# Mixture-of-experts stage of a hybrid encoder block: one result row per token, summed by the second expert's fetch

## The chip, the cores and the metric

The kernel runs on one core of one Trainium2 chip. The metric is the device time of one execution in microseconds. Three runs of the kernel before took 2249.4, 2248.95 and 2247.48 us, median 2248.95.

The engines are called by their usual short names: PE is TensorE, DVE is VectorE, ACT is ScalarE, POOL is GpSimd, SP is SyncE. A name such as L1415 is a line of the kernel.

## The reference

One layer over 2048 tokens of 1024 float32 values, `h`:

- `proj = h @ w_in`, 2048 columns: q, k, v of 8 heads and the input u of a bidirectional state-space model (S5).
- Neighbourhood attention over a 32 x 64 grid of tokens, S5 with GELU and GLU, both concatenated and multiplied by `w_out`; then `h = LayerNorm(alpha * h + mix)`.
- A hierarchical mixture of experts: each token chooses one of 8 groups, and in that group the two best of 8 experts. With gates g1 and g2:

```
hid_e = silu(x @ w_gate[e]) * (x @ w_up[e])      # 1024 -> 512
y     = g1 * (hid_e1 @ w_down[e1]) + g2 * (hid_e2 @ w_down[e2])
out   = LayerNorm(alpha * h + y)
```

Every token thus has two experts, both of the same group, and `alpha * h` has to be added once.

## The kernel before, in words

Work goes through five stages.

1. **Projection.** `w_in` comes in 16 chunks of 128 columns, in the hand-written `order`. SP loads a chunk (`load_w1`, L468) into a ring `rawp` of two raw buffers; ACT makes the high part (L445) and DVE the low part (L447) of the split that the three matmuls of `mm3` (L106 to L108) use. For each chunk four blocks `nb` of 512 tokens are computed, 24 matmuls each, into four PSUM tiles (`psA`). `evac` copies a block out, one block later: for the first four chunks (12 to 15, the u columns) ACT copies it (L489) into a staging tile of a pool with two buffers, and SP stores that to `ud` (L490). Chunk `n + 2` is loaded while chunk `n` is multiplied. At `n == 2` DVE fills one raw buffer with an out-of-range number (`sent`), and POOL's DMA queue copies it over the whole table `tab` (L755). The setup of S5 runs beside all this on DVE.
2. **Attention and S5**, then 3. **GLU, `w_out`, LayerNorm and router**, 128 tokens at a time. The normalized rows go to `hd` in device memory. `router_a` (L1149) finds the two experts `ef`, their gates and an entry `ent` of four words per choice: token row, output row, gate, factor of the residual. `router_b` (L1222) counts ranks within each expert and scatters the entries into `tab`, 96 slots (`SL`) for each expert; slots that stay unused keep the out-of-range number. For the last tile the index of the first expert's rows is taken from a matmul (`idx0`, L1244), so that the first gather (L1212) need not wait for `tab`.
4. **Experts.** Iteration `e` of the loop runs on POOL the gather of 96 rows of `hd` for expert e + 3 (L1212, six buffers `hg`), on PE gate and up of expert e, the transposes of expert e + 1 and down of expert e - 1; on ACT the residual scaling of expert e - 1 (L1400), on DVE the multiplication by the gate and the addition to the scaled rows (L1413); POOL scatters the rows to `yd` (L1415). `yd` has two rows per token: the first choice writes `alpha * h + g1 * y1`, the second `g2 * y2` (factor 0 for the residual). Weights come through a ring of 1 MB halves loaded by SP (L1106) in the order `seq_`; ACT (L1311) and DVE (L1317) split them for `mm3`. In iterations e = 6 to 26 POOL scatters one more small list (L1530), for a loop over experts with more than 96 tokens (L1535), which makes no turn with these inputs.
5. **Final stage.** SP loads both rows of 128 tokens (L1582, 1 MB a tile, 16 tiles, all issued at once), DVE adds them (L1593), ACT forms mean and variance (L1595, L1596) and the root (L1597), DVE scales (L1601 to L1603), two tiles later in program order, and POOL's queue stores (L1604).

The order of instructions on each engine is the order of the program; a DMA waits in its issuing engine's queue until its semaphores are there.

Of the kernel before, what the change touches and what calls it, by code (L numbers as in the profile page):

```python
# [12 lines left out]
F32 = mybir.dt.float32  # L13
F32R = mybir.dt.float32r
BF16 = mybir.dt.bfloat16
I32 = mybir.dt.int32
# [10 lines left out]
NE, DE = 64, 512  # L27
# [6 lines left out]
SPL = 1  # L34
NOT0 = 1 << 12
SL = 96
NBX = -(-SEQ // SL) - 1
NROW = SL * (NBX + 1)

# [33 lines left out]
def encoder_block(ctx: ExitStack, tc: tile.TileContext, A, out, dbg=None):  # L73
# [20 lines left out]
    md = dram.tile([G, C, 8, 128], F32, name="md")  # L94
    tbd = dram.tile([128, 2, G, 256], F32, name="tbd")
    hd = dram.tile([SEQ, DM], F32, name="hd")
    yd = dram.tile([2 * SEQ, DM], F32, name="yd")
    tab = dram.tile([NROW * NE, 4], I32, name="tab")
    lst = dram.tile([64, 4], I32, name="lst")

# [11 lines left out]
    GP.iota(io8, pattern=[[1, 8]], base=0, channel_multiplier=0, allow_small_or_imprecise_dtypes=True)  # L112
    io64 = const.tile([128, 64], F32, name="io64")
    GP.iota(io64, pattern=[[1, 64]], base=0, channel_multiplier=0, allow_small_or_imprecise_dtypes=True)
    tokf = const.tile([128, 16, 2, 2], I32, name="tokf")
    GP.iota(tokf, pattern=[[128, 16], [0, 2], [0, 2]], base=0, channel_multiplier=1)
    GP.iota(tokf[:, :, 1, 1:2], pattern=[[128, 16], [0, 1]], base=SEQ, channel_multiplier=1)
    alf = const.tile([128, 2], F32, name="alf")
    V.memset(alf[:, 0:1], ALPHA)
    V.memset(alf[:, 1:2], 0.0)  # L120
# [627 lines left out]
    for n, ch in enumerate(order):  # L748
        if n < 2:
            continue  # L750
        if n == 2:
            nfill = NROW * NE * 4 // 2048
            sent = rawp.tile([128, nfill], I32, name="sent", tag="raw")
            V.memset(sent, OOB)
            GP.dma_start(tab.rearrange("(p a b) w -> p a (b w)", p=128, a=16), sent[:, None, :].to_broadcast([128, 16, nfill]))  # L755
        hl = nxt
        for nb in range(4):
            ps = psA.tile([128, 512], F32, name="pp")
            for k in range(8):
                mm3(ps, (hl[:, 0, k, :], hl[:, 1, k, :]), (xs[nb][0][:, k, :], xs[nb][1][:, k, :]), k == 0, k == 7)  # L760
            if nb == SPL and n + 1 < len(order):
                nxt = split_chunk(order[n + 1])
            if nb == (max(2, SPL) if n == 2 else 0) and n + 2 < len(order):
                load_w1(order[n + 2])
            if n == 15:

                if nb == 0:
                    KT = [buf16([128, 2, ROWS, GW], F32R)]
                    QT = buf16([128, 2, SEQ], F32R)
                    load_k(0, 0)  # L770
                    load_k(0, 1)
                    load_q(0, 0)
                if nb == 1:
                    bts = buf16([128, 4, 2, 512])
                    KT.append(buf16([128, 2, ROWS, GW], F32R))
                    load_b()
                if nb == 2:
                    mixT = [buf16([128, 8, 512])]
                    for u in range(3):
# [304 lines left out]
        return A["w_" + nm][e].rearrange("(p j) f -> p j f", j=4 if nm == "down" else 8)  # L1084

    seq_ += [("gate", 0), ("up", 0)]
    for e in range(1, NE):
        seq_ += [("gate", e), ("up", e), ("down", e - 1)]
    seq_.append(("down", NE - 1))
    loaded, nsplit = [], [0]  # L1090
    ring, free, held = [], [], None

# [56 lines left out]
    def router_a(n, pr, res):  # L1149
# [48 lines left out]
        TS(dn, e2, 1.0, gs, ALU.add, ALU.mult)  # L1198
        ent = cw.tile([128, 2, 4], I32, name="ent", bufs=4)
        gt = ent.bitcast(F32)  # L1200
        V.tensor_copy(ent[:, :, 0:2], tokf[:, n])
        V.tensor_copy(gt[:, :, 3], alf)
        yield
        V.reciprocal(gt[:, 0, 2:3], dn)
        yield
# [5 lines left out]
    def gather(tb, hgt):  # L1211
        GP.indirect_dma_start(out=hgt[:SL], out_offset=None, in_=hd[:],  # L1212
                              in_offset=bass.IndirectOffsetOnAxis(ap=tb[:SL, 0:1], axis=0),
                              bounds_check=SEQ - 1, oob_is_err=False)

    def rank_m(oo):
        pr2 = psR.tile([128, 2, 64], F32, name="pr2")
# [4 lines left out]
    def router_b(pr2, ef, o2, oo, ent, val, n):  # L1222
# [16 lines left out]
            yield  # L1239
        row = cw.tile([128, 2], I32, name="row", bufs=4)  # L1240
        STT(row, rks, 64.0, ef, ALU.mult, ALU.add)
        yield
        if n == 15:
            TS(idx0[:SL], p0[:SL, 0:1], float(NOT0), None, ALU.add)  # L1244
# [167 lines left out]
    def down_out(tb, hgt, py, no_dep=True):  # L1412
        STT(hgt[:SL], py[:SL], tb[:SL, 2:3].bitcast(F32), hgt[:SL], ALU.mult, ALU.add)  # L1413
        GP.memset(spacer, 0.0)
        d = GP.indirect_dma_start(out=yd[:], out_offset=bass.IndirectOffsetOnAxis(ap=tb[:SL, 1:2], axis=0),  # L1415
                                  in_=hgt[:SL], in_offset=None, bounds_check=2 * SEQ - 1, oob_is_err=False)
        if no_dep:
            for o in ybufs:
                tc.declare_no_dep(d.ins, o.ins, reason="different rows")
            ybufs.append(d)  # L1420

    def down(hhl, get, tb, hgt, no_dep=True):
# [5 lines left out]
    def piece(nm, e, extra):  # L1428


        i = 4 * seq_.index((nm, e))
# [48 lines left out]
    for t_ in hg[1:]:  # L1480
        V.memset(t_, 0.0)
    for k in (1, 2):
        gather(tabs[:, k], hg[k])
    hid = None
    gb = None
    last = None
    for e in range(NE + 1):
# [4 lines left out]
            SY.dma_start(lng, A["ln2_g"].to_broadcast([128, DM]))  # L1492
            SY.dma_start(lnb, A["ln2_b"].to_broadcast([128, DM]))
        if e + 3 < NE:
            gather(tabs[:, e + 3], hg[(e + 3) % NHG])
        out_ = (tabs[:, e - 1], hg[(e - 1) % NHG]) if e else None
        if e < NE:
            get, after = piece("gate", e, {})
            pgt = up_mm(xhl, get, "g", after)
# [35 lines left out]
    with tc.For_i(0, nv, 1) as it:  # L1535
# [5 lines left out]
        SY.dma_start(tb[:SL], tab[bass.ds(rb_, SL, 64), :])  # L1541
        gather(tb, hg[0])
        xhl = trans_x(hg[0])

        nld = [0]

# [28 lines left out]
    fw = pf.enter_context(tc.tile_pool(name="fw", bufs=4))  # L1575
    ys = {}

    fy = [buf16([128, 2, 2, DM]) for _ in range(8)]

    def load_y(n):  # L1580
        ys[n] = fy[n // 2][:, n % 2]
        SY.dma_start(ys[n], yd.rearrange("(k t) d -> t k d", k=2)[128 * n:128 * n + 128])  # L1582

    eps = fp.tile([128, 1], F32, name="eps")
    V.memset(eps, EPS)
    for n in range(16):
        load_y(n)
    fin = {}
    for n in range(19):
        if n < 16:  # L1590
            y = ys.pop(n)
            h, junk = y[:, 0], y[:, 1]
            TT(h, h, junk, ALU.add)  # L1593
            mu, va = (fw.tile([128, 1], F32, name=f"m{c}") for c in "uv")
            S.activation(junk, h, AF.Copy, scale=-1.0 / DM, accum_out=mu)  # L1595
            S.activation(junk, h, AF.Square, bias=mu, accum_out=va)  # L1596
            S.activation(va, va, AF.Sqrt, bias=eps, scale=1.0 / DM)  # L1597
            fin[n] = h, mu, va
        if 2 <= n < 18:
            h, mu, va = fin.pop(n - 2)  # L1600
            V.reciprocal(va, va)  # L1601
            STT(h, h, mu, lng, ALU.add, ALU.mult)
            STT(h, h, va, lnb, ALU.mult, ALU.add)  # L1603
            GP.dma_start(out[128 * (n - 2):128 * (n - 2) + 128, :], h)  # L1604
    pf.close()
    if dbg:
        loc = dict(qd=qd, kd=kd, ud=ud, zd=zd, hd=hd, yd=yd, tab=tab)
# [66 lines left out]
```

## Time and profile before

| | before |
|---|---|
| median of three runs | 2248.95 us |
| the profiled execution's own time | 2250.54 us |
| its span in the trace | 2248.8 us |
| mean granted clock of TensorE, of full speed | 0.965 |
| PE busy | 2086.3 us (93%) |
| DVE busy | 1954.8 us (87%) |
| ACT busy | 1385.7 us (62%) |
| POOL busy | 524.8 us (23%) |
| DMA moved | 634.04 MB, mean 282 GB/s |

Busy times are from the profile's first section and overlap one another. A high share says only that an engine is full somewhere; which engine sets the pace in a stage has to be read from that stage. "DMA share" in a stretch is the mean busy share of the core's 16 DMA engines. In a row of a timeline the bracket at the end is the engine's idle time before the instruction and what ended it. "To landing" is the time from the issue of a DMA to its completion.

### The profile page before, as it was taken

How to read it: one execution, taken by the hardware profiler on the slowest of the kernel's cores; microseconds unless marked ns; L12 is line 12 of the kernel's file. 1: busy time of each engine (PE TensorE's matmuls, PEld its weight loads, DVE VectorE, ACT ScalarE, POOL GpSimd, SP SyncE). 2: the span in 40 equal slices, each digit the busy share in tenths (PEclk: the TensorE clock that was granted, in tenths of full speed). 3: DMA queues.
4: the chain of work that ended last, by engine and by line, in shares of the span. 5: the costliest groups of instructions: out<-in, count | busy, mean ns of one | idle time of the engine just before them, and what ended most of it. 6: DMA issues, size and time to landing. Idle time of an engine off the chain costs nothing. (4 is left out here: it accounts for less than half of the span.)

```text
span 2248.8 us, 31008 instructions
## 1 busy us (share of the span) xinstructions
PE 2086.3 (93%) x10653; PEld 1578.4 (70%) x10653; DVE 1954.8 (87%) x3573; ACT 1385.7 (62%) x1950; POOL 524.8 (23%) x408
## 2 busy tenths in 40 slices
PE   8999899999999999969999999999999999999940
PEld 6887677866666788856777777777777777777730
DVE  6976668999996778878999999999999999999967
ACT  4232221147778321127888888888888888888855
POOL 0001110010000011232244444443333333333211
PEclk9999899999999999979999999999999999999975
DMA  7435566599865433369999999999999999999647
GB/s 223 125 125 172 207 239 213 184 302 289 245 177 157 154 113 117 121 249 323 369 381 381 385 387 387 379 378 378 378 379 378 374 377 377 380 381 379 250 168 296
DMA packets 219887, 634.04 MB, mean 282 GB/s; under 512 B 39280, under 2 KB 119120, under 8 KB 170576
## 3 DMA queue, kind: packets, MB, share of 16 engines
q1 hardware_dynamic: 187424, 550.07, 68.3%
q0 software_dynamic: 32016, 81.40, 10.9%
q8 instruction: 85, 1.39, 0.3%
q10 hardware_dynamic: 288, 0.57, 0.1%
q14 instruction: 74, 0.61, 0.1%
HBM read 557.93 MB, written 100.26 MB: 293 GB/s over the span
## 5 line engine op out<-in xcount | busy, mean ns | idle before, releaser
L1317 DVE TENSOR_TENSOR b<-b,b 128x1024 fp32r<-128x1024 f32 x544 | 640.8, 1216 | 47.5 <-ACT b L1311 38.3
L1311 ACT ACTIVATE b<-b 128x1024 fp32r<-128x1024 f32 x544 | 576.0, 1059 | 144.1 <-PE pg L108 55.6
L1415 POOL DMA_INDIRECT yd<-hg,tabs x64 | 306.3, 4786 | 718.2 <-DVE hg L1413 689.1
L106 PE MATMUL pp<-b,whl 128*128 128x512 f32 (+1 forms) x520 | 210.0, 404 | 9.1 <-DVE b L447 8.3
L106 PE MATMUL pu<-b,xhl 128*96 128x512 f32 x512 | 206.0, 402 | 0.0
L108 PE MATMUL pg<-b,xhl 128*96 128x512 f32 x512 | 204.2, 399 | 1.7 <-DVE xhl L447 1.7
L106 PE MATMUL pg<-b,xhl 128*96 128x512 f32 x512 | 203.0, 396 | 2.6 <-ACT xhl L445 2.6
L107 PE MATMUL pp<-b,whl 128*128 128x512 f32 (+1 forms) x520 | 203.3, 391 | 1.2 <-DVE b L447 1.2
L108 PE MATMUL pp<-b,whl 128*128 128x512 f32 (+1 forms) x520 | 203.4, 391 | 0.5 <-DVE whl L447 0.5
L107 PE MATMUL pg<-b,xhl 128*96 128x512 f32 x512 | 202.6, 396 | 0.0
L106 PE MATMUL py<-b,hhl 128*96 128x512 f32 x504 | 202.1, 401 | 0.0
L108 PE MATMUL pu<-b,xhl 128*96 128x512 f32 x512 | 201.4, 393 | 0.0
L107 PE MATMUL pu<-b,xhl 128*96 128x512 f32 x512 | 200.9, 392 | 0.0
L108 PE MATMUL py<-b,hhl 128*96 128x512 f32 x504 | 198.0, 393 | 0.0
L107 PE MATMUL py<-b,hhl 128*96 128x512 f32 x504 | 197.5, 392 | 0.0
L1317 DVE TENSOR_TENSOR b<-half,b 128x1024 fp32r<-128x1024 f32 x132 | 157.1, 1216 | 11.3 <-ACT b L1311 8.9
L1311 ACT ACTIVATE b<-half 128x1024 fp32r<-128x1024 f32 x132 | 139.8, 1059 | 32.6 <-PE pg L108 11.5
L106 PEld LDWEIGHTS pp<-b,whl 128*128 128x128 f32 x520 | 99.7, 192 | 28.8 <-ACT b L445 8.3
L1317 DVE TENSOR_TENSOR b<-slot,b 128x1024 fp32r<-128x1024 f32 x92 | 109.0, 1216 | 7.8 <-ACT b L1311 6.1
L108 PEld LDWEIGHTS pp<-b,whl 128*128 128x128 f32 x520 | 99.5, 191 | 21.9 <-DVE whl L447 1.0
L107 PEld LDWEIGHTS pp<-b,whl 128*128 128x128 f32 x520 | 99.6, 192 | 21.3 <-DVE b L447 1.9
L108 PEld LDWEIGHTS pg<-b,xhl 128*96 128x96 f32 x512 | 83.3, 163 | 38.7 <-DVE xhl L447 2.8
(385 smaller groups left out, 4324.8 us busy)
## 6 DMA issues: line engine op xcount, KB each, us to landing
b<-in_w_up_dram SPq DMA_DIRECT2D x93, 1024.0 KB, 10.5
b<-in_w_gate_dram SPq DMA_DIRECT2D x90, 1024.0 KB, 8.6
b<-in_w_down_dram SPq DMA_DIRECT2D x88, 1024.0 KB, 9.1
half<-in_w_down_dram SPq DMA_DIRECT2D x23, 1024.0 KB, 8.8
half<-in_w_gate_dram SPq DMA_DIRECT2D x21, 1024.0 KB, 8.6
half<-in_w_up_dram SPq DMA_DIRECT2D x21, 1024.0 KB, 10.6
slot<-in_w_gate_dram SPq DMA_DIRECT2D x16, 1024.0 KB, 8.6
slot<-in_w_down_dram SPq DMA_DIRECT2D x16, 1024.0 KB, 9.2
```

Of the source, the lines that this page charges most:

```text
L106: T.matmul(o, l[0], r[0], start=start, stop=False)
L107: T.matmul(o, l[0], r[1], start=False, stop=False)
L108: T.matmul(o, l[1], r[0], start=False, stop=stop)
L1311: S.activation(wh[k % len(wh)][:, 0], src, AF.Copy, scale=1.0)
L1317: TT(hl[:, 1], src, hl[:, 0].bitcast(F32), ALU.subtract)
L1415: d = GP.indirect_dma_start(out=yd[:], out_offset=bass.IndirectOffsetOnAxis(ap=tb[:SL, 1:2], axis=0), in_=hgt[:SL], in_offset=None, bounds ...
```

## The change

- The experts are visited in the order `EO`: the first expert of each of the 8 groups, then the second of each, and so on. A token's two experts are then at least eight positions apart.
- `yd` has one row per token. It is filled once, at `n == 2` of the projection, with the bit pattern of the out-of-range number, which as float32 is a denormal next to zero; the transfer is issued by ACT, and `sent` grows from 264 to 1024 columns.
- `router_b` finds out which of the two choices comes second in the new order (`sec`; an overflowing slot counts as later). Its residual factor is 1 instead of alpha, and its entry's second word is the token's row; the first choice has a row out of range there.
- From e = 8 on, after the gather, `gather_sum` fetches rows of `yd` into `hg` for those slots that are a second choice, so that the residual scaled by 1 is the sum of the first expert. The scatter goes to the token's row for both choices.
- The final stage loads one row per token, 0.5 MB a tile, has no addition on DVE, and runs the scaling one tile after the statistics, not two.

The core of the diff:

```diff
+EO = [8 * (s % 8) + s // 8 for s in range(NE)]
...
-    yd = dram.tile([2 * SEQ, DM], F32, name="yd")
+    yd = dram.tile([SEQ, DM], F32, name="yd")
...
-            sent = rawp.tile([128, nfill], I32, name="sent", tag="raw")
+            sent = rawp.tile([128, DM], I32, name="sent", tag="raw")
             V.memset(sent, OOB)
...
+            S.dma_start(yd.rearrange("(p a) d -> p a d", p=128), sent.bitcast(F32)[:, None, :].to_broadcast([128, 16, DM]))
...
-    for e in range(1, NE):
-        seq_ += [("gate", e), ("up", e), ("down", e - 1)]
+    for s_ in range(1, NE):
+        seq_ += [("gate", EO[s_]), ("up", EO[s_]), ("down", EO[s_ - 1])]
...
-        V.tensor_copy(ent[:, :, 0:2], tokf[:, n])
-        V.tensor_copy(gt[:, :, 3], alf)
+        V.tensor_copy(ent[:, :, 0], tokf[:, n])
...
+    def gather_sum(tb, hgt):
+
+        return GP.indirect_dma_start(out=hgt[:SL], out_offset=None, in_=yd[:],
+                                     in_offset=bass.IndirectOffsetOnAxis(ap=tb[:SL, 1:2], axis=0),
+                                     bounds_check=SEQ - 1, oob_is_err=False)
...
+        sec = cw.tile([128, 2], F32, name="sec")
+        TS(sec, rks, SL - 0.5, 64.0, ALU.is_gt, ALU.mult)
+        yield
+        TT(ef, sec, ef, ALU.add)
+        yield
+        TT(sec, ef, ef[:, ::-1], ALU.is_gt)
+        yield
+        TS(ent.bitcast(F32)[:, :, 3], sec, 1.0 - ALPHA, ALPHA, ALU.mult, ALU.add)
+        STT(ent[:, :, 1], sec, -float(OOB), toko[:, n], ALU.mult, ALU.add)
...
-        d = GP.indirect_dma_start(out=yd[:], out_offset=bass.IndirectOffsetOnAxis(ap=tb[:SL, 1:2], axis=0),
-                                  in_=hgt[:SL], in_offset=None, bounds_check=2 * SEQ - 1, oob_is_err=False)
+        d = GP.indirect_dma_start(out=yd[:], out_offset=bass.IndirectOffsetOnAxis(ap=tb[:SL, 0:1], axis=0),
+                                  in_=hgt[:SL], in_offset=None, bounds_check=SEQ - 1, oob_is_err=False)
...
-            gather(tabs[:, e + 3], hg[(e + 3) % NHG])
+            gather(tabs[:, EO[e + 3]], hg[(e + 3) % NHG])
+        if 8 <= e < NE:
+            d = gather_sum(tabs[:, EO[e]], hg[e % NHG])
+            for o in ybufs[-6:]:
+                tc.declare_no_dep(d.ins, o.ins, reason="rows of other groups")
+            sums.append(d)
...
-        SY.dma_start(ys[n], yd.rearrange("(k t) d -> t k d", k=2)[128 * n:128 * n + 128])
+        SY.dma_start(ys[n], yd[128 * n:128 * n + 128, :])
...
-    for n in range(19):
+    for n in range(18):
         if n < 16:
-            y = ys.pop(n)
-            h, junk = y[:, 0], y[:, 1]
-            TT(h, h, junk, ALU.add)
+            h = ys.pop(n)
+            junk = fw.tile([128, DM], F32, name="junk", bufs=1)
...
-        if 2 <= n < 18:
-            h, mu, va = fin.pop(n - 2)
+        if 1 <= n < 17:
+            h, mu, va = fin.pop(n - 1)
```

What it moves shows in the instruction streams at three places. ACT in the projection, around the place where `sent` is set; `us` is the staging tile, `pp` a PSUM tile, `whl` the split chunk. Before:

```order
L445 ACTIVATE whl<-raw 128x1024 [waits DMAHW7_49,DVE_49,PE_49]
L489 COPY us<-pp 128x64x8 [waits DMAHW0_49,Activation_49]
L489 COPY us<-pp 128x64x8 [waits DMAHW1_49,Activation_49]
L489 COPY us<-pp 128x64x8 [waits DMAHW3_49,PE_49,Activation_49]
L445 ACTIVATE whl<-raw 128x1024 [waits DMAHW2_49,DVE_49]
L489 COPY us<-pp 128x64x8 [waits DMAHW4_49,PE_49,Activation_49]
```

and now:

```order
L445 ACTIVATE whl<-raw 128x1024 [waits DMAHW7_49,DVE_49,PE_49]
L489 COPY us<-pp 128x64x8 [waits DMAHW0_49,Activation_49]
L489 COPY us<-pp 128x64x8 [waits DMAHW1_49,Activation_49]
L757 DMA yd<-sent 2048x1x1024 [waits DVE_49]
L489 COPY us<-pp 128x64x8 [waits DMAHW3_49,PE_49,Activation_49]
L445 ACTIVATE whl<-raw 128x1024 [waits DMAHW2_49]
L489 COPY us<-pp 128x64x8 [waits DMAHW4_49,PE_49,Activation_49]
```

The fill stands between two copies out of PSUM and waits for DVE (the memset of `sent`).

SP's queue at the same place; `raw` is a buffer of the chunk ring, DMASW0 belongs to the table's fill on POOL's queue and, in the second piece, DMAHW5 to the fill of `yd`. Before:

```order
L490 DMA ud<-us 1024x1x64 [waits Activation_49] x2
L490 DMA ud<-us 1024x1x64 [waits DMAHW5_49,Activation_49]
L490 DMA ud<-us 1024x1x64 [waits DMAHW6_49,Activation_49]
L468 DMA raw<-in_w_in_dram 128x1024 [waits DMAHW7_49,DMAHW2_49,DVE_49]
L490 DMA ud<-us 1024x1x64 [waits DMAHW0_49,Activation_49]
L490 DMA ud<-us 1024x1x64 [waits DMAHW1_49,Activation_49]
L468 DMA raw<-in_w_in_dram 128x1024 [waits DMASW0_49]
L490 DMA ud<-us 1024x1x64 [waits DMAHW3_49,Activation_49]
```

and now:

```order
L490 DMA ud<-us 1024x1x64 [waits Activation_49] x2
L490 DMA ud<-us 1024x1x64 [waits DMAHW6_49,Activation_49]
L490 DMA ud<-us 1024x1x64 [waits DMAHW7_49,Activation_49]
L468 DMA raw<-in_w_in_dram 128x1024 [waits DMAHW0_49,DMAHW5_49,DMASW0_49,DVE_49]
L490 DMA ud<-us 1024x1x64 [waits DMAHW1_49,Activation_49]
L490 DMA ud<-us 1024x1x64 [waits DMAHW2_49,Activation_49]
L468 DMA raw<-in_w_in_dram 128x1024 [waits DMAHW3_49,DVE_49]
L490 DMA ud<-us 1024x1x64 [waits DMAHW4_49,Activation_49]
```

The chunk load that waits for the reader of `sent` was the second of the two shown; now it is the first, and it waits for both fills.

POOL in the expert stage, two iterations; `hg` are the six row buffers, `tabs` the expert's slots. Before:

```order
L1212 DMA hg_10002<-hd,tabs 96x1024 [waits DMASW6_49,DMASW3_49,PE_49]
L1414 MEMSET spacer 1x1 [waits Pool_49]
L1415 DMA yd<-hg_9998,tabs 4096x1024 [waits DVE_49]
L1212 DMA hg_7312<-hd,tabs 96x1024 [waits DMASW5_49,DMASW0_49,PE_49]
L1414 MEMSET spacer 1x1 [waits Pool_49]
L1415 DMA yd<-hg_9999,tabs 4096x1024 [waits DVE_49]
```

and now:

```order
L1213 DMA hg_7311<-hd,tabs 96x1024 [waits DMASW5_49,DMASW1_49]
L1219 DMA hg_10079<-yd,tabs 96x1024 [waits PE_49]
L1431 MEMSET spacer 1x1 [waits Pool_49]
L1432 DMA yd<-hg_10078,tabs 2048x1024 [waits DMASW3_49,DVE_49]
L1213 DMA hg_10077<-hd,tabs 96x1024 [waits DMASW4_49,DMASW0_49]
L1219 DMA hg_10080<-yd,tabs 96x1024 [waits PE_49]
L1431 MEMSET spacer 1x1 [waits Pool_49]
L1432 DMA yd<-hg_10079,tabs 2048x1024 [waits DMASW6_49,DVE_49]
```

Each iteration has one more indirect transfer, between the gather and the memset ahead of the scatter, and it waits for PE (the transposes that read the buffer).

## Rows read from the trace of the kernel before

**Rows 1.** Busy time by stretches: PE, PEld, DVE, ACT, POOL, clock, DMA share, GB/s.

```profile
60.00:100.00 40.00, 40.00 (x178) 33.14 (x177) 37.66 (x195) 8.55 (x8) 1.28 (x1) 1.00 0.51 135
240.00:300.00 60.00, 50.65 (x245) 40.05 (x244) 44.40 (x100) 14.46 (x40) 7.49 (x14) 0.89 0.60 206
1200.00:1600.00 400.00, 400.00 (x1869) 289.06 (x1868) 378.58 (x357) 333.50 (x356) 160.30 (x83) 1.00 1.01 382
2100.00:2140.00 40.00, 40.00 (x187) 28.80 (x186) 38.05 (x36) 33.09 (x36) 10.29 (x4) 1.00 0.44 164
2180.00:2220.00 40.00, 0.00 (x0) 0.00 (x0) 39.07 (x43) 30.58 (x58) 5.42 (x10) 0.50 1.02 415
```

**Rows 2.** Timeline of DVE in the final stage (start us, us, line, op, names).

```profile
2180.58 1.23 DVE L1593 TENSOR_TENSOR b<-b 128x1024 f32<-128x1024 f32 x1 [1.34 <-DMA b<-yd]
...
2228.85 1.22 DVE L1593 TENSOR_TENSOR b<-b 128x1024 f32<-128x1024 f32 x1
...
2232.56 0.15 DVE L1601 RECIPROCAL mv<-mv 128x1 f32<-128x1 f32 x1
...
2235.14 0.16 DVE L1601 RECIPROCAL mv<-mv 128x1 f32<-128x1 f32 x1
...
2236.51 1.28 DVE L1603 SCALAR_TENSOR_TENSOR b<-b,mv,slot 128x1024 f32<-128x1024 f32 x1
```

**Rows 3.** Timeline of ACT, the first tiles of the final stage.

```profile
2176.19 1.06 ACT L1595 ACTIVATE b<-b 128x1024 f32<-128x1024 f32 x1 [19.96 <-DVE b L1593]
...
2180.13 1.04 ACT L1595 ACTIVATE b<-b 128x1024 f32<-128x1024 f32 x1
...
2182.77 1.04 ACT L1595 ACTIVATE b<-b 128x1024 f32<-128x1024 f32 x1
```

**Rows 4.** The loads L1582 by their source line, on SP's queue.

```profile
L1582 SPq DMA_DIRECT2D b<-yd x16: 395/1896/7597, 2169.8 to 2200.5; - x16
...
DMA to landing us min/median/max: 5.1/21.4/29.0
```

**Rows 5.** Timeline of POOL, two stretches of the expert stage.

```profile
1283.06 1.30 POOL L1530 DMA_INDIRECT lst<-ent_l,rows_l  x1 [0.30 <-issue]
...
1301.04 1.29 POOL L1530 DMA_INDIRECT lst<-ent_l,rows_l  x1 [0.30 <-issue]
...
2056.09 1.35 POOL L1212 DMA_INDIRECT hg<-hd,tabs  x1 [0.30 <-issue]
...
2074.09 1.35 POOL L1212 DMA_INDIRECT hg<-hd,tabs  x1 [0.30 <-issue]
```

**Rows 6.** Timeline of ACT in an iteration; the scatter L1415 by its source line.

```profile
2075.89 1.14 ACT L1400 ACTIVATE hg<-hg,tabs 96x1024 f32<-96x1024 f32 x1
...
DMA to landing us min/median/max: 3.6/12.0/13.8
```

**Rows 7.** Waits of SP's queue: us in total, times, longest.

```profile
SPq L1106 <- DVE b L1317: 971.3, 367, 14.4
```

**Rows 8.** Timelines of DVE and of TensorE, last router tile.

```profile
988.03 0.17 DVE L1187 CAST ef<-j 128x2 f32<-128x2 uint32 x1
988.23 0.16 DVE L1189 SCALAR_TENSOR_TENSOR ef<-gf,ef 128x2 f32<-128x2 f32 x1
...
998.77 1.07 PE L1365 MATMUL px<-ident,hg 96*128 96x96 f32 x5 [7.71 <-DMA hg<-hd,idx]
```

**Rows 9.** Timelines of SP, ACT, POOL, projection; the table's fill L755 by its source line.

```profile
69.95 0.33 SPq L468 DMA_DIRECT2D raw<-in_w_in_dram  x1
...
74.23 1.09 ACT L489 COPY us<-pp 128x512 f32<-128x512 f32 x1 [4.33 <-PE pp L108]
79.67 1.09 ACT L489 COPY us<-pp 128x512 f32<-128x512 f32 x1 [4.35 <-PE pp L108]
...
65.50 1.28 POOL L755 DMA_DIRECT2D tab<-sent  x1 [63.07 <-DVE st L254]
...
DMA to landing us min/median/max: 9.7/9.7/9.7
```

More of the change, by code (lines that the diff above doesn't have):

```diff
@@ L114, in encoder_block @@
     GP.iota(io64, pattern=[[1, 64]], base=0, channel_multiplier=0, allow_small_or_imprecise_dtypes=True)
[L115 to L120, printed above, removed]
+    tokf = const.tile([128, 16, 2], I32, name="tokf")
+    GP.iota(tokf, pattern=[[128, 16], [0, 2]], base=0, channel_multiplier=1)
+    toko = const.tile([128, 16, 2], F32, name="toko")
+    GP.iota(toko, pattern=[[128, 16], [0, 2]], base=OOB, channel_multiplier=1, allow_small_or_imprecise_dtypes=True)
     tri = const.tile([128, 128], BF16, name="tri")
@@ L752, in encoder_block @@
             nfill = NROW * NE * 4 // 2048
-            sent = rawp.tile([128, nfill], I32, name="sent", tag="raw")
+            sent = rawp.tile([128, DM], I32, name="sent", tag="raw")
             V.memset(sent, OOB)
-            GP.dma_start(tab.rearrange("(p a b) w -> p a (b w)", p=128, a=16), sent[:, None, :].to_broadcast([128, 16, nfill]))
+            GP.dma_start(tab.rearrange("(p a b) w -> p a (b w)", p=128, a=16), sent[:, None, :nfill].to_broadcast([128, 16, nfill]))
+            S.dma_start(yd.rearrange("(p a) d -> p a d", p=128), sent.bitcast(F32)[:, None, :].to_broadcast([128, 16, DM]))
         hl = nxt
@@ L1086, in encoder_block @@
     seq_ += [("gate", 0), ("up", 0)]
-    for e in range(1, NE):
-        seq_ += [("gate", e), ("up", e), ("down", e - 1)]
-    seq_.append(("down", NE - 1))
+    for s_ in range(1, NE):
+        seq_ += [("gate", EO[s_]), ("up", EO[s_]), ("down", EO[s_ - 1])]
+    seq_.append(("down", EO[NE - 1]))
     loaded, nsplit = [], [0]
@@ L1414, in down_out @@
         GP.memset(spacer, 0.0)
-        d = GP.indirect_dma_start(out=yd[:], out_offset=bass.IndirectOffsetOnAxis(ap=tb[:SL, 1:2], axis=0),
-                                  in_=hgt[:SL], in_offset=None, bounds_check=2 * SEQ - 1, oob_is_err=False)
+        d = GP.indirect_dma_start(out=yd[:], out_offset=bass.IndirectOffsetOnAxis(ap=tb[:SL, 0:1], axis=0),
+                                  in_=hgt[:SL], in_offset=None, bounds_check=SEQ - 1, oob_is_err=False)
         if no_dep:
             for o in ybufs:
-                tc.declare_no_dep(d.ins, o.ins, reason="different rows")
+                tc.declare_no_dep(d.ins, o.ins, reason="different rows, or ordered by the sum's way")
+            for o in sums[-6:]:
+                tc.declare_no_dep(d.ins, o.ins, reason="rows of other groups")
             ybufs.append(d)
@@ L1428, in piece @@
     def piece(nm, e, extra):
-        i = 4 * seq_.index((nm, e))
+        i = 4 * seq_.index((nm, EO[e]))
         def after(q):
@@ L1482, in encoder_block @@
     for k in (1, 2):
-        gather(tabs[:, k], hg[k])
+        gather(tabs[:, EO[k]], hg[k])
+    sums = []
     hid = None
@@ L1494, in encoder_block @@
         if e + 3 < NE:
-            gather(tabs[:, e + 3], hg[(e + 3) % NHG])
-        out_ = (tabs[:, e - 1], hg[(e - 1) % NHG]) if e else None
+            gather(tabs[:, EO[e + 3]], hg[(e + 3) % NHG])
+        if 8 <= e < NE:
+            d = gather_sum(tabs[:, EO[e]], hg[e % NHG])
+            for o in ybufs[-6:]:
+                tc.declare_no_dep(d.ins, o.ins, reason="rows of other groups")
+            sums.append(d)
+        out_ = (tabs[:, EO[e - 1]], hg[(e - 1) % NHG]) if e else None
         if e < NE:
@@ L1543, in encoder_block @@
         xhl = trans_x(hg[0])
+        gather_sum(tb, hg[0])
         nld = [0]
@@ L1576, in encoder_block @@
     ys = {}
-    fy = [buf16([128, 2, 2, DM]) for _ in range(8)]
+    fy = [buf16([128, 4, DM]) for _ in range(4)]
     def load_y(n):
-        ys[n] = fy[n // 2][:, n % 2]
-        SY.dma_start(ys[n], yd.rearrange("(k t) d -> t k d", k=2)[128 * n:128 * n + 128])
+        ys[n] = fy[n // 4][:, n % 4]
+        SY.dma_start(ys[n], yd[128 * n:128 * n + 128, :])
     eps = fp.tile([128, 1], F32, name="eps")
@@ L1603, in encoder_block @@
             STT(h, h, va, lnb, ALU.mult, ALU.add)
-            GP.dma_start(out[128 * (n - 2):128 * (n - 2) + 128, :], h)
+            GP.dma_start(out[128 * (n - 1):128 * (n - 1) + 128, :], h)
     pf.close()
```

## The prediction

> **What bounds the kernel now.** I read the page's shares first (TensorE busy in 93% of the span), then busy time by stretches, then the places that the change touches. Only stretches in which TensorE is not busy, or is made to wait, can move the end; the second view tells which they are [rows 1]. In 60 to 100 (the projection) and 1200 to 1600 (the experts) TensorE is busy all the time at granted clock 1.00. In 1200 to 1600 DVE has 378.58 of 400 us and the DMA share is 1.01 at 382 GB/s too, so three resources are full at once, and TensorE, which never pauses, sets the pace. In 2180 to 2220 TensorE does nothing, DVE has 39.07 of 40 us and the DMA share is 1.02 at 415 GB/s: the final stage is bounded by DVE, with DMA close behind.
>
> **The final stage: removed work.** On DVE the adds L1593 of tile 3 and tile 16 start at 2180.58 and 2228.85 [rows 2]: 48.27 us for 13 tiles, 3.71 each (add, reciprocal, two multiplies). The last two tiles have no add beside them and take 2235.14 - 2232.56 = 2.58. The last multiply ends at 2236.51 + 1.28 = 2237.79, 11.0 us before the span's end (last store and exit), which I leave as it is. Without the add DVE needs 2.58 a tile and is no longer the slowest: ACT's two passes, unhindered, repeat after 2182.77 - 2180.13 = 2.64 us, and the first tile takes 3.94 (2176.19 to 2180.13), with a table load in it [rows 3]. DMA moves 0.52 MB in and 0.52 MB out per tile, 1.05 MB at 415 GB/s = 2.53 us, just under it. So ACT is the new bound at 2.64.
>
> Start: the first load goes out at 2169.8, and the shortest of these 1 MB loads lands after 5.1 us [rows 4]. Half of it lands after between 2.6 us (all in proportion) and 5.1; I take 3.85, the middle, since a fixed part and a rate are both in it. ACT then starts at about 2173.7 instead of 2176.2, with no add to wait for. Its 16 tiles end at 2173.7 + 3.94 + 15 x 2.64 = 2217.2; reciprocal and multiplies of the last tile add 2237.79 - 2235.14 = 2.65: 2219.9 against 2237.8, **-17.9 us** (-16.6 to -19.1 by the start alone; -15.5 if the transfers slow ACT to 2.8 a tile).
>
> **The experts: added fetches and a new order.** Which expert comes when changes only the addresses of loads. Added are 56 indirect fetches on POOL, one per iteration from e = 8, right behind the gather for e + 3. POOL has room: where the small list scatter L1530 stands ahead of the gather (1283.06, 1301.04), an iteration has three indirect transfers and lasts 17.98 us; with two (gathers L1212 at 2056.09, 2074.09) it lasts 18.00 [rows 5]. With three, POOL is busy for 160.30 of 400 us [rows 1]. I take 1.35 us of POOL for a fetch, the gather's row: nothing on the path.
>
> The fetch also puts a wait in front of the residual scaling on ACT (L1400), behind which the hi splits of the next weights are queued, and DVE and TensorE wait for those. The fetch behind the gather at 2056.09 would go out at about 2057.7; its tile's scaling stands in the next iteration, at 2075.89 [rows 6]: 18.2 us. The nearest transfer, the indirect scatter of such a tile to the same tensor, lands after 3.6, 12.0 and 13.8 us (least, median, most) [rows 6]. The margin is 4 us at worst: **0 us**; beyond 18.2 each further microsecond would be paid.
>
> Bytes: 2048 rows of 4 KB, 8.39 MB, at 382 GB/s 22 us of all DMA engines, beside weight loads that keep them full. What hides them is that the loads run ahead: SP spent 971.3 us of them waiting for DVE to free a buffer [rows 7], and in 2100 to 2140 the DMA share is down to 0.44 while TensorE stays at 40 of 40 us [rows 1], so the loads are through some 40 us before the matmuls are. 22 fit in that: **0 us** (ends: 0 and +22).
>
> The Trainium skill ("DMA: Bandwidth & Descriptors", Specifications) gives about 358 GB/s as a core's limit to HBM. The trace goes past it, at 382 and 415 GB/s [rows 1]. By that figure the fetched bytes would be an estimated 23.4 us, and the final stage would be held by DMA at 2.9 us a tile, its term some 4 us smaller; I stay with the rows.
>
> **The router.** Five small DVE operations per tile are new and one copy goes. Dependent ones of this size follow each other by 0.20 us (988.03, 988.23) [rows 8]. In 15 of 16 tiles TensorE is busy beside them. In the last they stand before the index that the first gather needs, and TensorE waits 7.71 us for that gather, until 998.77 [rows 8]. Four dependent steps make 0.8; the copies of the tiles just before, handled together with it, I put at 0.2: **+1.0 us** (0.5 to 1.5).
>
> **The fill of yd: an added transfer in the projection.** The 8.39 MB fill goes out on ACT's queue when its source tile is set, where POOL fills the table now: 65.50, landing 9.7 us later for 2.1 MB [rows 9]. Both fills make 10.5 MB, 25.3 us at 415 GB/s; the table's alone would be 5.1 us at that rate, so 4.6 us are fixed. The fill thus lands at about 66 + 25.3 + 4.6 = 96. It collides at one place: its source is a buffer of the ring of w_in chunks, and in the new order the chunk load that went out at 69.95 [rows 9] waits for it, with two stores of u behind it on SP. All three go out 26 us late. ACT's copies out of PSUM write staging tiles, of which there are two, so the copy at 79.67 now waits for the first of those stores, until 96 + 4 = 100, and ends at 101. TensorE has four accumulators, and blocks follow each other every 5.44 us (copies at 74.23 and 79.67, each at a block's end [rows 9]); the block that needs this copy would start at 74.23 + 4 x 5.44 = 96.0, and starts at 102: 6 us late. The late chunk itself lands about 101 and is split some 2.5 us later; its first block was due at 101.4, so this falls into the same delay. TensorE is at 40 of 40 us there, so a delay is carried to the end. A pause also costs clock: in 240 to 300 TensorE is idle for 9.35 us and the granted clock has a mean of 0.89 [rows 1], 6.6 us of full speed lost on top. For 6 us I take 3, since the pause may come in pieces, and 1 back where TensorE waits later anyway: 6 + 3 - 1 = **+8 us** (ends: +1, if the fill finds gaps between other transfers and lands before 80, and +18, below).
>
> **Sum.** -17.9 + 0 + 0 + 1.0 + 8 = -8.9. The profiled execution took 2250.54, so 2241.6; the median of the runs, 2248.95, is 1.6 lower, and with that off it is 2240. Faster or slower counts from 0.2%, 4.5 us, about what a measurement of this kernel can tell from no change.
>
> **Rivals.**
> *The fill is hidden* (+1 instead of +8): the DMA share in 60 to 100 is 0.51 [rows 1], so half of the engines' time is free. Against it: one chunk load waits for all of the fill. 2233. Chance 0.14.
> *The fill blocks more.* It stands on ACT between two copies; while its descriptors don't fit into the queue ACT stands too, and no copy frees an accumulator. DVE waits for the late chunk with the S5 work behind it, which TensorE wants later. A pause of 11 us in one piece and 7 of clock, +18: 2250. Chance 0.17.
> *Slower: the fetches take the weights' time.* If the loads are 40 us ahead only at the end of the stage and not all through it, the 22 us of bytes come out as waits of TensorE, from the point on where a load lands after its split is due. The share of 1.01 speaks for it, SP's 971.3 us against it. -8.9 + 22 = +13.1: 2262. Chance 0.09.
> *Slower: fetches land late.* If reads of rows take over 18.2 us, 1 us over in 30 of the 56 is +30, 2270. The 13.8 us of the slowest scatter speak against it. Chance 0.06.
> *The change does not do what it says:* if slots that have nothing to fetch are moved all the same, 56 x 96 rows are 22 MB, 58 us of DMA and some 18 over the lead: 2258. For it: only the index tells the two apart. Chance 0.02.
>
> **How the numbers follow.** The forecast, 2240, has 0.52, with its own range 2234 to 2247 (fill +3 to +13, tail -15.5 to -19). Below 2244.5 are nine tenths of it (0.47), the hidden fill (0.14) and a little of the blocking one (0.03): faster 0.64. Same: the rest of the forecast and most of the blocking fill, 0.19. Slower: late or costly fetches and empty slots, 0.17. The range goes from below the hidden fill to beyond the blocking one, 2231 to 2254, and leaves out the slower cases.
>
> **What would show it.** Right: in the final stage ACT L1595 without a wait for DVE, 2.64 us a tile, 46 us from the first of them to DVE's last multiply; in the expert stage TensorE full and 17.98 us an iteration; in the projection a pause near 96 to 102, with a chunk load issued near 96. Wrong: TensorE pauses between 1200 and 2100, an ACT wait for a DMA at L1400, or a tail of 2.9 us a tile with a DMA share of 1.0.

## The result and the profile after

| | before | changed |
|---|---|---|
| median of four runs each | 2248.94 us | 2263.82 us (2261.09 to 2264.45) |
| profiled execution: own time | 2250.54 us | 2264.45 us |
| its span | 2248.8 us | 2262.7 us |
| mean granted clock | 0.965 | 0.971 |
| DMA moved | 634.04 MB | 642.46 MB |

The ratio is 1.0065, 95% interval 1.0048 to 1.0082: the changed kernel is 14.9 us slower. The forecast was 2240, faster, with a range up to 2254.

The span is best compared at a few marks that both traces have. Timeline of TensorE in the changed kernel, the first transposes of gathered rows and the last transposes of the expert stage:

```profile
1007.10 0.43 PE L1382 MATMUL px<-ident,hg 96*128 96x96 f32 x1 [8.90 <-DMA hg<-hd,idx]
...
2192.14 0.61 PE L1410 MATMUL phd<-ident,hid 96*128 96x96 f32 x4
```

and the second of these in the kernel before:

```profile
2153.56 0.61 PE L1393 MATMUL phd<-ident,hid 96*128 96x96 f32 x4
```

The first mark stood at 998.77 [rows 8], so the expert stage starts 8.3 us late. Of that, the wait for the gather accounts for 8.90 - 7.71 = 1.2, the router's part, and 7.1 are older. They come from the projection: from the 97th of its matmuls (`pp`) to the 385th it took 65.28 us before and takes 75.23 now, 9.95 more, and some of that is not left when the experts begin. The last mark is 38.6 us late, so the experts themselves lost 38.6 - 8.3 = 30.3. Busy time by stretches says where (columns as in [rows 1]: PE, PEld, DVE, ACT, POOL, clock, DMA share, GB/s):

```profile
60.00:100.00 40.00, 32.62 (x134) 26.22 (x133) 25.78 (x118) 5.01 (x5) 1.29 (x1) 0.91 0.83 295
1200.00:1600.00 400.00, 400.00 (x1873) 289.41 (x1872) 377.87 (x356) 334.49 (x357) 185.19 (x110) 1.00 1.01 376
1600.00:2000.00 400.00, 390.18 (x1799) 276.84 (x1797) 362.83 (x342) 316.78 (x342) 168.21 (x84) 1.00 1.00 357
2000.00:2100.00 100.00, 93.64 (x421) 64.44 (x421) 86.06 (x81) 74.66 (x81) 49.96 (x20) 1.00 1.00 358
2100.00:2140.00 40.00, 37.15 (x167) 25.53 (x167) 33.36 (x32) 27.75 (x31) 10.18 (x8) 1.00 1.00 352
2215.00:2250.00 35.00, 0.00 (x0) 0.00 (x0) 34.54 (x40) 34.13 (x68) 7.01 (x13) 0.50 0.86 342
```

and the kernel before in the two stretches of the expert stage that were not shown:

```profile
1600.00:2000.00 400.00, 400.00 (x1871) 289.18 (x1870) 378.59 (x357) 333.81 (x356) 146.11 (x67) 1.00 1.01 378
2000.00:2100.00 100.00, 100.00 (x469) 72.33 (x468) 94.15 (x90) 84.01 (x90) 35.77 (x18) 1.00 1.02 380
```

In 60 to 100 TensorE has 32.62 of 40 us and a mean clock of 0.91. In 1200 to 1600 TensorE is as full as in [rows 1], with 1873 matmuls. Then the count falls from 1871 to 1799, from 469 to 421, and from 187 to 167 [rows 1]. That is 140 matmuls of 400 / 1871 = 0.214 us, 30 us of work, though the busy time drops by only 19 us: the pauses are many and small, and the count shows them better. Meanwhile the DMA share stays at 1.00 to the end of the experts (before, 0.44 in 2100 to 2140 [rows 1]), at 357 GB/s instead of 378. The last row is the final stage: ACT and DVE are both full, at 34.13 and 34.54 of 35 us, and DMA has room at 0.86.

What TensorE waits for there, in the view of waits from 1836 to 2200 (us in total, times, longest):

```profile
PE pg L109 <- DVE b L1334: 12.3, 16, 1.0
PE py L109 <- DVE b L1334: 2.7, 7, 0.8
PE pu L109 <- DVE b L1334: 2.4, 4, 0.8
```

and ACT in the same stretch:

```profile
ACT b L1328 <- DMA b<-in_w_gate_dram: 15.2, 9, 3.2
ACT b L1328 <- DMA b<-in_w_up_dram: 11.6, 15, 2.8
ACT b L1328 <- DMA b<-in_w_down_dram: 10.2, 7, 3.1
```

From 1100 to 1836 TensorE has a single wait,

```profile
PE pu L109 <- DVE b L1334: 0.3, 1, 0.3
```

and the three rows above make 17.4 us after that. From then on ACT waits for weight loads, DVE's second half of the split comes late behind it, and TensorE behind that. The weight loads by their source line (L1108, before L1106): what ACT waited for them (us, times), and the time from issue to landing:

```profile
  ACT b L1328: 58.0, 51
...
DMA to landing us min/median/max: 4.9/22.7/30.7
```

and before:

```profile
DMA to landing us min/median/max: 4.8/9.1/13.5
```

The median went from 9.1 to 22.7 us. SP's waits show that the lead is gone:

```profile
SPq L1108 <- DVE b L1334: 462.6, 197, 15.1
...
SPq L1108 <- DMA b<-in_w_gate_dram: 131.0, 49, 4.8
```

The 971.3 us in which SP waited for DVE to free a buffer [rows 7] are 462.6 now. Instead SP waits for earlier weight loads to land, in nine such rows of which this is the largest, 573.8 us in all. The fetch itself lands in time, at most 15.4 us after its issue against the 18.2 that it has, and ACT's scaling (L1417) shows no wait for it:

```profile
L1219 POOL DMA_INDIRECT hg<-yd,tabs x56: 962/1036/5702, 1167.8 to 2184.6; - x56
...
DMA to landing us min/median/max: 7.7/11.7/15.4
```

The projection in the timeline of ACT, with the fill and the copies out of PSUM:

```profile
64.96 0.58 ACTq L757 DMA_DIRECT2D yd<-sent  x1
...
67.50 1.08 ACT L489 COPY us<-pp 128x512 f32<-128x512 f32 x1
90.27 1.02 ACT L489 COPY us<-pp 128x512 f32<-128x512 f32 x1 [21.69 <-DMA ud<-us]
97.95 1.07 ACT L489 COPY us<-pp 128x512 f32<-128x512 f32 x1 [6.67 <-DMA ud<-us]
```

of TensorE, around its pause:

```profile
83.60 0.39 PE L110 MATMUL pp<-b,whl 128*128 128x512 f32 x1
91.34 0.80 PE L108 MATMUL pp<-b,whl 128*128 128x512 f32 x1 [7.35 <-ACT us L489]
```

and of SP, the two stores of u and then the chunk load that waits for the fill:

```profile
66.77 2.35 SPq L490 DMA_DIRECT2D ud<-us  x2
96.18 0.33 SPq L468 DMA_DIRECT2D raw<-in_w_in_dram  x1
```

The fill is issued at 64.96 and lands 31.1 us later, at 96.1, and the chunk load goes out at 96.18, all as forecast. But TensorE already stops at 83.6 (the last matmul starts at 83.60, the next at 91.34 after a wait of 7.35). It waits for ACT's copy at 90.27, and that for a store of u, issued at 66.77, before SP came to the chunk load at all. The two stores issued there landed after 23.4 and 29.2 us; by their source line the least, median and most went from 2.8, 3.1 and 7.3 us before to 2.8, 3.8 and 29.2. The copy at 97.95 waited for the other one.

The final stage in the timeline of ACT, the first pass of the first three tiles:

```profile
2210.26 1.06 ACT L1620 ACTIVATE junk<-b 128x1024 f32<-128x1024 f32 x1 [15.45 <-DMA b<-yd]
...
2214.19 1.04 ACT L1620 ACTIVATE junk<-b 128x1024 f32<-128x1024 f32 x1
...
2216.83 1.04 ACT L1620 ACTIVATE junk<-b 128x1024 f32<-128x1024 f32 x1
```

of DVE, its last instruction:

```profile
2255.34 1.28 DVE L1628 SCALAR_TENSOR_TENSOR b<-b,mv,slot 128x1024 f32<-128x1024 f32 x1
```

and of SP, the loads:

```profile
L1608 SPq DMA_DIRECT2D b<-yd x16: 319/383/642, 2206.8 to 2219.7; - x16
```

The first load goes out at 2206.8 (2169.8 [rows 4]), 37.0 us late. That is 1.6 less than at the last transposes, above all because six of the last matmuls took 0.63 us each before (at 2157.32 to 2159.46) and all of them take 0.39 to 0.47 now. From the first load to DVE's last end it took 2237.79 - 2169.8 = 68.0 before [rows 2, 4] and 2256.62 - 2206.8 = 49.8 now: -18.2. What is left to the span's end was 11.0 and is 6.1; POOL's closing DRAIN (median and longest in ns) takes 4.96 us now

```profile
L1695 POOLq DRAIN  x3: 46/110/4957, 2256.9 to 2262.4; - x3
```

and took 9.87 before:

```profile
L1670 POOLq DRAIN  x3: 46/110/9867, 2238.1 to 2248.5; - x3
```

In sum 7.1 + 1.2 + 30.3 - 1.6 - 18.2 - 4.9 = +13.9, the difference of the spans.

### The profile page after: what moved, and what is told of

Its sections match the earlier page's. It is cut to its first block, busy times and chain, and to the rows that moved or that the text cites. A ratio compares the mean times of both kernels' runs of the same rounds, so it can differ in the third digit from the quotient of the medians.

```text
span 2262.7 us, 31201 instructions
## 1 busy us (share of the span) xinstructions
PE 2097.0 (93%) x10653; PEld 1575.8 (70%) x10653; DVE 1946.6 (86%) x3619; ACT 1378.1 (61%) x1950; POOL 605.0 (27%) x464
## 2 busy tenths in 40 slices
DMA packets 226176, 642.46 MB, mean 284 GB/s; under 512 B 43520, under 2 KB 123360, under 8 KB 176864
## 5 line engine op out<-in xcount | busy, mean ns | idle before, releaser
L108 PEld LDWEIGHTS pp<-b,whl 128*128 128x128 f32 x520 | 100.0, 192 | 36.1 <-ACT us L489 8.2
L1328 ACT ACTIVATE b<-slot 128x1024 fp32r<-128x1024 f32 x92 | 96.2, 1057 | 32.1 <-DVE b L1334 6.7
L109 PEld LDWEIGHTS pp<-b,whl 128*128 128x128 f32 x520 | 100.1, 193 | 21.1 <-DVE b L447 1.7
## 6 DMA issues: line engine op xcount, KB each, us to landing
b<-in_w_gate_dram SPq DMA_DIRECT2D x90, 1024.0 KB, 22.7
half<-in_w_down_dram SPq DMA_DIRECT2D x23, 1024.0 KB, 22.7
```

The source lines that it names most:

```text
L108: T.matmul(o, l[0], r[0], start=start, stop=False)
L109: T.matmul(o, l[0], r[1], start=False, stop=False)
L1328: S.activation(wh[k % len(wh)][:, 0], src, AF.Copy, scale=1.0)
```

## The experiments

The theory after the result, called 'uneven' in the expectations: the fetched rows take time from the weight loads at some of the 16 DMA engines, namely those that carry the low slots. An expert's list is filled from slot 0 and has 64 of 96 slots in use on average (4096 assignments on 64 experts), so gather, scatter and fetch all lie on the same engines; a weight load is complete only when its slowest engine is. The rivals: all engines are short of time, and it is the bytes as such; the new order of the weights in memory; something about reading `yd` while it is being written; the wait at the residual. Times are medians; each ratio is to the kernel before, run beside it on the same chip. Its median was 2247.2 to 2248.9 on the chips used, so differences between kernels of different groups of runs carry up to 1.7 us of that: the kernels without the fetches, with another order of weights and with the fill elsewhere ran together, then those with the slots spread and with `hd`, then the last three.

**Without the fetches.** The changed kernel with

```diff
-        if 8 <= e < NE:
+        if False:
```

> The changed kernel without the 56 fetches L1219 (the second expert's rows are then not summed with the first's); new expert order, fill and final stage stay. Theory 'bytes' (the 8.39 MB that the fetches read overload DMA): the expert stage runs as before, first gate matmul to last down 17.98 us an iteration, weight loads land in about 9 us, total 2264 - 30 = about 2234. Theory 'order' (the weights' addresses in the new order make the loads slower): expert stage still at about 355 GB/s late in the stage, total 2255 to 2264. Theory 'edge' (each alone fits, only both together do not): 2234 to 2240.

Measured 2240.2 us, ratio 0.9968 (0.9956 to 0.9981), 23.6 less than with them. The stretch 1600 to 2000:

```profile
1600.00:2000.00 400.00, 400.00 (x1872) 289.13 (x1872) 378.03 (x357) 334.39 (x357) 142.94 (x66) 1.00 1.01 379
```

TensorE is full again and the loads land after 4.8, 9.5 and 12.8 us. From the last router matmul to the last transposes it is 1164.54 us, 1194.56 with the fetches and 1163.13 before: the fetches cost 30.0 in the expert stage. (The difference of the medians is smaller, mostly by the DRAIN, which is 9.87 us without fetches.)

**The order of the weights.** The changed kernel with the weights taken from memory in the old order (the edit shown), and the kernel before with them in the new one (the same line, with the order turned round):

```diff
-        return A["w_" + nm][e].rearrange(...)
+        return A["w_" + nm][EO.index(e)].rearrange(...)
```

> The changed kernel with its fetches, but the weights are read in their stored order (position s reads expert s's weights, so experts compute with other experts' weights); slots, gathers and fetches as in the change. Theory 'bytes': no difference, about 2264, DMA about 357 GB/s in 1600 to 2000. Theory 'order': DMA back at 380 GB/s or above, loads landing in 10 to 15 us, total about 2234. Theory 'edge': 2234 to 2245.

> The kernel before, in which only the weights are read in the new order (experts compute with other experts' weights); no fetch, no fill, old final stage. Theory 'bytes': no difference, about 2249, load landing 9 us. Theory 'order': the expert stage gets longer by 15 to 30 us, 2264 to 2279. Theory 'edge': about 2249, with load landing times above 9 us but no wait of TensorE.

Measured 2264.5, ratio 1.0074 (1.0057 to 1.0091), and 2249.29, ratio 1.0004 (0.9994 to 1.0013). The order of the weights does nothing, alone or with the fetches.

**The fill elsewhere.** `sent` keeps its 264 columns; the fill goes out in four quarters from a zeroed row buffer, on ACT's queue, in the router's stage:

```diff
-            S.dma_start(yd.rearrange(...), sent.bitcast(F32)[:, None, :].to_broadcast([128, 16, DM]))
...
+        if n in (2, 4, 6, 8):
+            q = slice(2 * n - 4, 2 * n)
+            S.dma_start(yd.rearrange("(p a) d -> p a d", p=128)[:, q], hg0[:, None, :].to_broadcast([128, 4, DM]))
```

> The changed kernel with the fill of yd taken out of the projection: four quarters of 2.1 MB are written from the zeroed tile hg0 while the router stage runs (tiles 2, 4, 6, 8). If the fill's cost is the 7.35 us pause of TensorE at 83.6 (a staging tile's store that lands 23 us late behind the fill) and the half clock after it, the expert stage starts 7 us earlier and the total is about 2257. Rival: the quarters delay the x tiles and weight loads there, and the gain is given back: 2262 to 2266.

Measured 2255.25, ratio 1.0038 (1.0024 to 1.0052), 8.6 less than the changed kernel. The projection and the stretch of the experts:

```profile
60.00:120.00 60.00, 60.00 (x268) 49.65 (x268) 54.89 (x241) 13.03 (x17) 1.29 (x1) 1.00 0.41 114
1600.00:2000.00 400.00, 391.08 (x1809) 278.37 (x1808) 365.48 (x343) 317.71 (x344) 175.35 (x88) 1.00 1.00 359
```

The projection has no pause now, and the first gathered rows reach TensorE at 997.35. The loss in the experts is as it was.

**Reading another tensor.** The fetch reads `hd` in place of `yd`:

```diff
-        return GP.indirect_dma_start(out=hgt[:SL], out_offset=None, in_=yd[:],
+        return GP.indirect_dma_start(out=hgt[:SL], out_offset=None, in_=hd[:],
```

> The change with its fetches reading the same rows of hd instead of yd (so the first expert's result is lost). Theory 'yd' (reading a tensor that the scatters write at the same time is what is slow): about 2240. Theories 'uneven' and 'bytes': 2264, since engines, rows and bytes are the same.

Measured 2265.07, ratio 1.0071 (1.0054 to 1.0088); in 1600 to 2000 TensorE has 1803 matmuls at 360 GB/s. It has nothing to do with `yd` or with reading behind the scatters.

**The slots spread out.** The test of the theory: rank r of an expert goes to slot 6 (r mod 16) + r div 16 in place of slot r, so that empty slots lie everywhere. Bytes, instructions and waits stay the same; the slots' table is loaded in six pieces.

```diff
-    GP.iota(slots, pattern=[[1, SL]], base=0, channel_multiplier=0, ...)
+    GP.iota(slots, pattern=[[1, 16], [16, 6]], base=0, channel_multiplier=0, ...)
...
-    SY.dma_start(tabs[:SL], tab[0:SL * 64, :].rearrange("(s e) w -> s e w", e=64))
+    for b in range(6):
+        SY.dma_start(tabs[b:SL:6], tab[1024 * b:1024 * b + 1024, :].rearrange("(s e) w -> s e w", e=64))
```

In the changed kernel alone:

> The change as it is (fill in the projection) with the slots spread, nothing else. Theory 'uneven': 2264 - 24 = about 2240, as without the fetches. Theory 'bytes': 2264.

in the kernel before:

> The kernel before with the slots spread in the same way, nothing else. Both theories: TensorE bounds its expert stage, total about 2248 (up to 4 us more for six loads of the slots' table instead of one). Theory 'uneven': weight loads land in 5 to 7 us instead of 9 and the DMA share in 1200 to 2000 falls below 1.0; theory 'bytes': landing and share as before.

and in the changed kernel together with the fill moved:

> The changed kernel with the fill in the router stage and the ranks of an expert's tokens dealt out over the 96 slots (slot 6a + b holds rank 16b + a) instead of in a row, so that the occupied slots, on average 64 of 96, are spread over all partitions. Theory 'uneven' (rows of the indirect transfers fall on some of the 16 DMA engines, those of the low slots, and these engines are the ones that run full): weight loads land within 8 to 12 us, first and last engine of a load within 5 us, TensorE never waits in 1200 to 2140, total about 2231. Theory 'bytes' (all engines are full, the fetched bytes cost what they cost): no difference to the same kernel without the spread, 2255.

Alone it gave 2234.89, ratio 0.9940 (0.9923 to 0.9957): 28.9 us less than the changed kernel, with every fetch in place. Its stretches:

```profile
1600.00:2000.00 400.00, 400.00 (x1870) 288.92 (x1869) 378.51 (x357) 334.11 (x357) 164.50 (x88) 1.00 1.02 384
2000.00:2100.00 100.00, 100.00 (x467) 72.20 (x466) 95.16 (x90) 83.14 (x90) 41.12 (x22) 1.00 1.02 384
```

and SP's wait for buffers in it:

```profile
SPq L1108 <- DVE b L1334: 892.5, 348, 15.1
```

The same bytes go through at 384 GB/s, TensorE is full, and SP waits 892.5 us for buffers. In the kernel before the same edit gave 2247.88, ratio 0.9996 (0.9986 to 1.0005): no time, though the loads landed after 5.0, 7.4 and 9.8 us instead of 4.8, 9.1 and 13.5. The fall of the DMA share below 1.0 that 'uneven' expected there did not come: it is 1.01 as before. With the fill moved it is 2226.52, ratio 0.9901 (0.9884 to 0.9917), 8.4 less than the spread alone.

The trace also has the time at which each of the 16 engines reported its part of a transfer. One weight load and one gather near 1925, us after the issue, in order of size:

```
before
1926.9 weights  5.1 5.1 5.2 5.2 5.2 5.2 5.3 5.6 5.7 5.9 6.3 6.6 6.6 6.7 7.0 8.5
1930.3 gather   5.2 5.5 5.5 5.5 5.6 6.1 8.8 8.9 9.2 9.5 9.5 10.0 10.2 10.2 10.3 10.6
changed
1924.8 weights  5.6 5.7 6.1 6.5 7.1 8.2 9.6 10.2 10.8 18.3 23.4 24.0 24.7 29.4 29.7 29.8
1926.4 gather   4.3 4.4 6.0 6.2 6.2 8.1 10.3 10.4 10.8 11.0 11.0 11.2 11.2 11.4 11.4 11.5
changed, slots spread
1928.8 weights  6.8 7.5 8.1 8.1 8.6 9.5 9.7 9.7 10.0 11.7 12.9 13.2 14.7 17.8 18.3 18.4
1937.9 gather   8.8 8.9 9.0 9.0 9.1 9.3 9.3 9.3 9.4 9.4 9.5 9.5 9.5 9.6 9.7 9.7
```

In the changed kernel nine engines are done with the weights within 10.8 us and seven need up to 19 more. A gather already showed two kinds of engines before, six at 5 to 6 us and ten at 9 to 11; with the slots spread its 16 parts end within 0.9 us of one another. An estimate: if each engine had six slots in a row, 64 used slots would give ten to eleven engines something to do, and with the spread each would have four of its six; the two kinds fit that, but no run shows it.

The loads are much like these examples. Over those issued between 1650 and 2080 whose 16 reports are all on record, the last part of a weight load comes 20.8 us after the first in the median in the changed kernel (132 loads), 4.2 before (144) and 11.0 with the slots spread (130). In the kernel before the spread takes 4.2 to 2.0. So it evens the parts, but with the fetches not to the 5 us that had been expected. The Trainium skill ("DMA: Bandwidth & Descriptors", Why a DMA increments its semaphore by 16 and not by 1) says that a transfer runs on up to 16 engines that finish independently and is complete when the last has reported; the lists agree.

**What the fetches cost with the slots spread.** The last kernel but without fetches:

> Spread slots, fill in the router stage, but without the 56 fetches (second rows not summed). What is left of the fetches' price once the slots are spread: theory 'uneven': nothing up to the last down matmul (the same time from the first gate matmul to it, within 1 us, as with the fetches). Rival 'half': the spread only shortens the queues and the fetched bytes still cost some 5 to 10 us. POOL's last drain was 9.87 us in the four kernels without fetches and 4.96 in the six with them, so the total should be up to 5 us longer than with the fetches: 2226 to 2231.

Measured 2228.84, ratio 0.9923 (0.9908 to 0.9938). From the last router matmul to the last transposes it is 1162.76 us, and 1163.16 with the fetches: their price is 0.4 us here, 30.0 above. This speaks against the rival 'half' (5 to 10 us).

**The closing DRAIN.** The last stores issued from SP in place of POOL (L1629, before L1604), on top of the spread and the moved fill, and in the kernel before:

```diff
-            GP.dma_start(out[128 * (n - 1):128 * (n - 1) + 128, :], h)
+            SY.dma_start(out[128 * (n - 1):128 * (n - 1) + 128, :], h)
```

> Spread slots, fill in the router stage, fetches, and the final stage's 16 stores issued from SP instead of POOL. Theory 'drain' (POOL's drain at the end of the program takes 4.96 us after its last store and ends after the store has landed): POOL's drain runs early and the end comes right after the last store's landing, -1.5 us, 2225. Rival (the end waits for the landing and SP's own drain as long): no change, 2226.5.

> The kernel before with only its 16 final stores issued from SP instead of POOL, behind the loads. Theory 'drain' (9.87 us of POOL's drain after the last store, against 3 us until it lands): -6 us, 2242.5. Rival (stores held behind SP's load issues give the gain back): 2248.

Measured 2221.94, ratio 0.9890 (0.9875 to 0.9905), and 2240.59, ratio 0.9970 (0.9959 to 0.9982): 4.6 (3.4, each against its own kernel before) and 6.6 us less than without this edit. The DRAIN in the first of them:

```profile
L1698 POOLq DRAIN  x3: 46/104/2772, 2166.0 to 2219.6; - x3
```

and in the second:

```profile
L1670 POOLq DRAIN  x3: 46/104/7998, 2167.8 to 2239.0; - x3
```

The long one now runs early, at 2166.0 and 2167.8, beside the final stage. 2221.94 us is the fastest version of this study, 1.1% under the kernel before. From DVE's last end to the span's end it is 2219.8 - 2216.24 = 3.6 us against 2226.3 - 2220.25 = 6.1 with the stores on POOL, so 2.5 us are the DRAIN's. The rest of the gain lies ahead of the experts, where the first gathered rows reach TensorE at 995.78 in the one and at 1000.04 in the other; the edit does nothing there, and why these two executions differ is open.

## Why the prediction was wrong

**Bytes: "22 fit in that: 0 us".** This is the step that failed. It took the 16 DMA engines as one pool that moves 382 GB/s with a lead of 40 us, and put 22 us of bytes into the lead. The lead is real: it hides the fetches to 0.4 us when they are spread. But the share of 1.01 did not mean that DMA was full: with the slots spread the fetches go through beside the weights, and TensorE keeps its pace. Nor does a mean over 16 engines tell how they differ, and a load has landed when the last of its 16 parts has. In the changed kernel seven of the 16 parts of a load came up to 19 us after the others, the lead was gone by about 1836, and the rest of the stage ran at their pace: +30.3 in place of 0. That the place of the rows in their tile makes the price is shown by the spread alone, which took 28.9 us back. That the place acts through the engines is read from the 16 reports, which do not name them; the spread also moves the rows to other partitions of SBUF, the on-chip memory that they are loaded into, and no run separates the two. A hint was there before: the gather's parts came in two groups 3 us apart.

**The nearest rival** was the fetches taking the weights' time, +22, 2262, at 0.09. Its sign and place (loads landing after their split is due, from some point on) are what happened, and its total is within 2 us of the result. Its price was not: +22 came from all engines' bytes, the loss was 30.3, and the total agrees only because the tail gave 6.8 more than forecast (0.3 + 1.6 + 4.9) and the fill cost 0.9 less. Its mechanism as I put it, bytes as such, falls with the spread slots, which move the same bytes without loss.

**The rate of 357 GB/s** of the changed kernel stands close to the 358 that the Trainium skill gives as a core's limit to HBM ("DMA: Bandwidth & Descriptors", Specifications). It is no limit here: the same transfers go at 384 GB/s with the slots spread, and DMA in the final stage before ran at 415 [rows 1].

**The fill: +8, measured +7.1** between the two profiled executions, and 8.6 and 8.4 by the medians when it was moved. In the projection itself it is 9.95, and nearly the same in all traces: 65.28 us between the same two matmuls in each of the eight kernels without the fill there, 75.22 to 75.59 in the five with it. The size was right, the place and the cause were not, so that the agreement is luck. I had it through the late chunk load, with a pause at 96 to 102. The chunk load went out when I said and stopped nobody; the pause came at 83.6, since two small stores of u that were issued just behind the fill landed 23 and 29 us later. Nor did ACT stand at the fill, as the rival of the blocking fill had it: its issue took 0.58 us. I looked for instructions behind a wait and not for transfers behind a transfer. The Trainium skill says that DMAs issued by different engines run on the same 16 DMA engines and interleave ("DMA: Bandwidth & Descriptors", Issuing engines are not separate DMA queues); the trace agrees, and has the price.

**The router: +1.0, measured +1.2.** Right, as a longer wait for the first gather. Over all traces with the slots in a row that wait is 8.47 to 8.90 us with the new steps and 7.71 to 8.11 without, so some 0.9.

**The final stage: -17.9, measured -18.2.** Right: DVE has no add, ACT repeats every 2216.83 - 2214.19 = 2.64 us, and its first tile starts at 2210.26, 3.5 us after the first load's issue, against the 3.85 taken. Left out were the 1.6 of clock just before it and the DRAIN, "which I leave as it is".

**The fetches' landing: 0, right.** 15.4 us at most against 18.2. The rival of late fetches had its budget right and does not occur; nor are empty slots moved: without the fetches the changed kernel moves 634.04 MB, so they bring 642.46 - 634.04 = 8.42 MB, one reading of the 2048 rows.

## What to carry to other kernels

Where DMA runs all the time, ask where in the tile the rows of an indirect transfer lie, and not only how many bytes it moves: here rows in the low slots of partly filled tiles held up seven of the 16 parts of the regular loads, each of which waits for its last part, and the mean share of busy time showed none of it. Spreading the valid rows over the tile costs nothing and gave back 28.9 us here. And before a large transfer is put into a stage with gaps, look at which small transfers of that stage are on a short loop, such as the stores that free a staging tile: here they came back at the large one's pace, not at their own.

## What the runs showed of the hardware

- Stores of u that land after 3.1 us in the median took 23.4 and 29.2 us when issued just behind a fill of 8.39 MB on another engine's queue.
- POOL's closing DRAIN took 9.87 us in the five kernels without fetches that store from POOL, 4.96 to 4.97 in the six with them, and lies beside other work if POOL's last DMA comes earlier. Why it is 9.87 or 4.96 is open.
- Also open: which engine serves which slot (the trace has 16 reports, not their owners), whether it is the engines or the side of SBUF that the low slots load unevenly, and why the weight load in the last of the three lists still has nine early and seven late parts (from 11.7 us on) though the slots are spread, so that the rows' place is not all that makes engines unequal. With the stores on SP the loads landed after 4.9, 10.7 and 27.7 us, and TensorE was full all the same. A fill from a source tile of its own, in the projection, was not tried.
